# A four-layer hybrid trunk in split float32r: products regrouped by stationary weight, and mixer B's glu and value columns in shared slabs

## The chip, the cores and the metric

The kernel runs on one core of one Trainium2 chip. The metric is the device time of one execution in microseconds, the median over runs; lower is better. TensorE (PE) multiplies, VectorE (DVE) and ScalarE (ACT) work from SBUF and PSUM, GpSimd (POOL) works from SBUF, and the DMA queues bring the weights from HBM. PSUM has eight banks of 512 float32 columns.

## What is computed

The trunk has four residual layers over 256 tokens of 2048 features: mixer A (dilated windowed attention), B (gated convolution), C (retention), then A again, and a closing RMSNorm. The large products are the input and output projections.

```python
for i in range(4):                       # kinds A, B, C, A
    h = rmsnorm(x, norm_w[i])
    x = x + mixer(h)
# mixer B
val, glu_gate, gate = split(h @ w_in, 3)          # 2048 columns each
c = causal_conv31(val * sigmoid(glu_gate)) + conv_b
y = (silu(layernorm(c)) * silu(gate)) @ w_out
```

Mixer A forms q, k (both turned by a rotary table) and v for three dilation groups of eight heads of 128, takes a banded softmax, multiplies by silu(gate) and projects out. Mixer C forms q, k, v and a gate for eight heads, runs a chunked decaying recurrence, normalises each head and projects out.

## The kernel before

**Precision.** Every weight and every activation that enters a projection is split in two float32r parts, high and low (`wh`, `wl`; `xh`, `xl`). A product of two such operands is three matmuls: high by high, high by low, low by high. Each matmul has a weight load of its own (LDWEIGHTS, "PEld" in the profile).

**The stream of slabs.** The weights are read once, as 368 slabs of 1 MB. A `Piece` (L46) is one slab with its matmuls. The main loop (L1064 to the end of the loop) walks the slabs in order: the slab's matmuls, then `cut(i + 2)` (L1049: ACT copies `raw` to `wh` at L1058, DVE or POOL subtracts to `wl` at L1059, and the load of the slab three on is issued by SP at L1047), then the slab's eviction `after`, then side work out of the queues `side`, `slow` and `rare`. `pop` (L114) lets side work in up to a budget in microseconds per slab. Since the program order of every engine is this order, an instruction that waits holds up whatever was written behind it on its engine.

**Three ways to multiply.** `mm_ws` (L137) keeps a 128x128 block of W stationary and streams the 256 tokens, feature-major result, two blocks in a bank; `chunk_ws` and `group_ws` use it (matmuls at L153, L154, L155). `mm_xs` (L175) keeps x stationary and streams 512 weight columns, one bank for each half of the tokens (L187 to L189). `mm_xs2` (L158) keeps x stationary and streams 256 weight columns, both token halves in one bank (L168, L170, L171); only mixer B's first 16 slabs use it.

**PSUM.** `ps_acc` (L65) has four tiles of one bank, `ps_s` and `ps_t` two each.

**Mixer A, q and k.** `after_qk` (L475) evicts two heads with one DVE product by the per-token 1/rms (L479), shuffles the 32 rotary rows (L481), and POOL does the rotation in three steps (L482, L483, L484). After the last k chunk of a head pair, `attention` pushes seven groups of side work; the first of them, after the next slab's matmuls, multiplies q by k (L498 for the first dilation group, L501 for the others).

**Mixer B.** 48 slabs of input projection: for pairs 0 to 3 two 256-wide glu slabs and two 256-wide value slabs each, for pairs 4 to 7 512-wide ones, two pairs at a time; then 16 gate slabs. The eviction of the glu part applies a sigmoid (L684, ACT), that of the value part multiplies (L694, DVE, put in `slow`), `turn` (L672) transposes on PE (L677) and ACT copies to a padded buffer (L678). `conv` (L710) then pushes 31 taps for each pair as side work: tap 0 on ACT (L724), taps 1 to 30 on DVE (L726), each tap one instruction for each of two feature blocks `j`. The accumulators lie in PSUM:

```python
st["ps"] = [(ps_t if c % 2 else ps_s)() for _ in range(2)]
acc = [b[:, 0:S] for b in st["ps"]]      # one bank for each j
...
V.scalar_tensor_tensor(acc[j], src, w, acc[j], op0=OP.mult, op1=OP.add)
```

The budget (L27, 4.7 us; 5.5 in most gate slabs) admits six, later seven taps for each slab. From slab 6 to 45 POOL makes `wl`. When pair 7 is convolved, a LayerNorm over the features follows (L786 to L827: sums on PE at L792, moments, then eight steps that make the operands `big` of the output projection), and the 16 output slabs (`group_ws`) start when the first of these are there. `defer_first` (L226) puts the statistics of the layer's RMSNorm behind the first chunk and that chunk's eviction behind the next slab.

**Residual.** `new_x` (L280) adds a branch of 256 features to x with one DVE instruction (L282) and splits the result for the next layer.

## Time and profile before

| what | value |
|---|---|
| median of 3 runs | 2276.22 us (2275.72 to 2276.3) |
| profiled execution, from first to last instruction | 2275.0 us (its own run time is not recorded) |
| PE busy | 2219.7 us, 98% of the span, 14996 matmuls |
| DVE busy | 1330.0 us, 58% |
| ACT busy | 980.6 us, 43% |
| POOL busy | 553.0 us, 24% |
| DMA | 395.95 MB, mean 174 GB/s |
| granted TensorE clock, mean over the span | 0.994 |

A busy share is a mean over the stages. The layers follow one another: A to about 576 us, B to about 969, C to about 1727, A to the end. PE's matmuls overlap in the records (a 256-column one shows 0.28 us), so their cost is read from the distance between the starts of neighbours, not from their durations. The granted clock has two levels here, 1.00 (2.4 GHz) and 0.50 (1.2 GHz).

### The profile page before, as it was taken

To read this page: it belongs to the slowest core of one execution; us is meant where nothing else is said; L and a number is where in the kernel's file an instruction comes from. 1 tells how busy PE (TensorE), PEld (TensorE's weight loads), DVE (VectorE), ACT (ScalarE), POOL (GpSimd) and SP (SyncE) were. 2 spreads that over 40 slices of the span, in tenths; PEclk is the share of its full clock that TensorE was granted. 3 is DMA by queue.
4 is the path that set the end of the run, shared out by engine and by line. 5 is a ranking of instruction groups with operands and counts; after the bars stand their busy time and mean duration, and the time that the engine had idled before them with its cause. 6 is when DMAs were issued, how large, how long until landed. Compare 5 with 4: busy or idle time off the path is not lost.

```text
span 2275.0 us, 34524 instructions
## 1 busy us (share of the span) xinstructions
PE 2219.7 (98%) x14996; PEld 2059.6 (91%) x14996; DVE 1330.0 (58%) x1536; ACT 980.6 (43%) x913; POOL 553.0 (24%) x273
## 2 busy tenths in 40 slices
PE   6999999999999997999999999999999999999998
PEld 5889999999998887999889889899988889999996
DVE  5545655556597886565455455455555446555554
ACT  4433333345434444444443444344366333333353
POOL 3004344321488973110000000000000005334311
PEclk9999999999999998999999999999999999999999
DMA  6655455445555553555565555555555555455444
GB/s 194 199 198 186 149 167 167 149 148 186 167 185 185 180 172 127 189 182 177 173 201 171 193 181 167 192 183 169 190 169 170 197 187 184 149 167 165 154 145 148
DMA packets 301376, 395.95 MB, mean 174 GB/s; under 512 B 6567, under 2 KB 212775, under 8 KB 301221
## 3 DMA queue, kind: packets, MB, share of 16 engines
q1 hardware_dynamic: 299232, 391.14, 52.7%
q8 instruction: 117, 1.92, 0.4%
q10 hardware_dynamic: 1592, 1.93, 0.2%
q0 software_dynamic: 400, 0.67, 0.2%
q14 instruction: 35, 0.28, 0.0%
HBM read 391.63 MB, written 2.10 MB: 173 GB/s over the span
## 4 chain that ended last, share of the span: by engine, by line
PE 91%; DVE 3%; POOL 2%; DMA 2%; ACT 1%; issue 1%; SPq 0%; DVEq 0%; ACTq 0%; POOLq 0%
PE ps_acc L155 16%; PE ps_acc L154 16%; PE ps_acc L153 16%; PE ps_acc L188 11%; PE ps_acc L187 11%; PE ps_acc L189 11%; PE ps_acc L171 1%; PE ps_acc L168 1%; PE ps_acc L170 1%; PE ps_t L534 1%; POOL tmp L483 1%; DMA xin<-in_x_dram 1%; DVE wl L1059 1%; PE ps_t L969 1%; DMA raw<-in_a_w_in_dram 1%
## 5 line engine op out<-in xcount | busy, mean ns | idle before, releaser
L1059 DVE TENSOR_TENSOR wl<-raw,wh 128x2048 fp32r<-128x2048 f32 (+1 forms) x329 | 781.8, 2378 | 567.1 <-ACT wh L1058 564.8
L1058 ACT ACTIVATE wh<-raw 128x2048 fp32r<-128x2048 f32 (+1 forms) x371 | 703.4, 1898 | 716.6 <-PE ps_acc L154 342.0
L153 PE MATMUL ps_acc<-xhl,wh 128*128 128x256 f32 x2304 | 656.9, 285 | 0.0
L154 PE MATMUL ps_acc<-xhl,wh 128*128 128x256 f32 x2304 | 651.9, 283 | 0.1
L155 PE MATMUL ps_acc<-xhl,wl 128*128 128x256 f32 x2304 | 652.0, 283 | 0.0
L187 PE MATMUL ps_acc<-wh,xhl 128*128 128x512 f32 x1152 | 453.0, 393 | 0.0
L188 PE MATMUL ps_acc<-wl,xhl 128*128 128x512 f32 x1152 | 449.8, 390 | 0.4 <-DVE wl L1059 0.4
L189 PE MATMUL ps_acc<-wh,xhl 128*128 128x512 f32 x1152 | 449.8, 390 | 0.0
L154 PEld LDWEIGHTS ps_acc<-xhl,wh 128*128 128x128 f32 x2304 | 442.0, 192 | 0.7 <-DVE xhl L306 0.3
L153 PEld LDWEIGHTS ps_acc<-xhl,wh 128*128 128x128 f32 x2304 | 442.0, 192 | 0.4
L155 PEld LDWEIGHTS ps_acc<-xhl,wl 128*128 128x128 f32 x2304 | 441.8, 192 | 0.0
L189 PEld LDWEIGHTS ps_acc<-wh,xhl 128*128 128x128 f32 x1152 | 217.1, 188 | 45.9
L188 PEld LDWEIGHTS ps_acc<-wl,xhl 128*128 128x128 f32 x1152 | 217.4, 189 | 44.6 <-DVE wl L1059 0.7
L187 PEld LDWEIGHTS ps_acc<-wh,xhl 128*128 128x128 f32 x1152 | 217.3, 189 | 44.1
L1059 POOL TENSOR_TENSOR wl<-raw,wh 128x2048 fp32r<-128x2048 f32 x42 | 194.7, 4637 | 69.7 <-ACT wh L1058 53.4
L482 POOL TENSOR_TENSOR qk<-qk,ropeA 32x512 f32<-32x512 f32 x48 | 63.6, 1326 | 607.5 <-DVE tmp L481 607.5
L274 POOL COPY ssq<-tmp 128x512 f32<-128x512 f32 x4 | 5.4, 1352 | 836.1 <-ACT tmp L299 812.5
L153 PE MATMUL ps_acc<-z,wh 128*128 128x256 f32 x512 | 145.4, 284 | 0.0
L155 PE MATMUL ps_acc<-z,wl 128*128 128x256 f32 x512 | 145.1, 283 | 0.0
L154 PE MATMUL ps_acc<-z,wh 128*128 128x256 f32 x512 | 144.6, 282 | 0.0
L483 POOL TENSOR_TENSOR tmp<-tmp,ropeA 32x512 f32<-32x512 f32 x48 | 121.0, 2520 | 0.0
L726 DVE SCALAR_TENSOR_TENSOR ps_s<-u,bw,ps_s 128x256 f32<-128x256 f32 x232 | 91.8, 481 | 26.2 <-ACT ps_s L724 26.2
(227 smaller groups left out, 2596.7 us busy)
## 6 DMA issues: line engine op xcount, KB each, us to landing
raw<-in_a_w_in_dram SPq DMA_DIRECT2D x160, 1024.0 KB
raw<-in_c_w_in_dram SPq DMA_DIRECT2D x96, 1024.0 KB
raw<-in_b_w_in_dram SPq DMA_DIRECT2D x48, 1024.0 KB
raw<-in_c_w_out_dram SPq DMA_DIRECT2D x32, 1024.0 KB
raw<-in_a_w_out_dram SPq DMA_DIRECT2D x16, 1024.0 KB
raw<-in_b_w_out_dram SPq DMA_DIRECT2D x16, 1024.0 KB
xin<-in_x_dram SPq DMA_DIRECT2D x16, 128.0 KB
out_dram<-qk SPq DMA_DIRECT2D x8, 256.0 KB
```

The source lines that it names most:

```text
L153: T.matmul(ps, w_h, xh, start=st, stop=False, skip_group_check=True)
L154: T.matmul(ps, w_h, xl, start=False, stop=False, skip_group_check=True)
L155: T.matmul(ps, w_l, xh, start=False, stop=last and i == kk - 1, skip_group_check=True)
L168: T.matmul(ps, xh, wh[:, i, :], start=p == 0 and t == 0 and i == 0, stop=False, skip_group_check=True)
L187: T.matmul(ps, xh, wh[:, i, :], start=p == 0 and i == 0, stop=False)
L188: T.matmul(ps, xh, wl[:, i, :], start=False, stop=False)
L189: T.matmul(ps, xl, wh[:, i, :], start=False, stop=p == np_ - 1 and i == kk - 1)
L482: G.tensor_tensor(q[:32], q[:32], ropeA[:, 0:1].to_broadcast([32, 2, S]), op=OP.mult)
L483: G.tensor_tensor(sw, sw, ropeA[:, 1:2].to_broadcast([32, 2, S]), op=OP.mult)
L726: V.scalar_tensor_tensor(ct[:, j] if k == TAPS - 1 else acc[j], src, w, acc[j], op0=OP.mult, op1=OP.add)
L1058: A.activation(wh[:, sl], r[:, sl], AF.Copy)
L1059: (V if p.lo == "v" else G).tensor_tensor(wl[:, sl], r[:, sl], wh[:, sl].bitcast(F32), op=OP.subtract)
```

## The change

`mm_ws` streams both parts of x in one 512-column matmul against the stationary high weight block, into a whole bank (high by high in the left half, high by low in the right), and then the high part of x in a 256-column matmul against the low weight block, into the right half. The two halves are added on eviction: `joined` copies the right half with ACT and adds the left with DVE; `new_x` adds both halves to x with two DVE instructions. `ps_acc` becomes two tiles of two banks. q is no longer multiplied by the 1/rms in `after_qk` (k still is); the factor goes into the scale of the softmax's exponential. `group_ws`, used by mixer B's output projection alone, keeps three 256-column matmuls as `mm_wg`, with the K tiles outermost in its first slab.

In mixer B, `mm_xs2` goes: every pair has four slabs of 512 columns, 256 of value beside 256 of glu, loaded by two DMAs each. `turn` takes its bank from `ps_s`, `conv` has both accumulators of a pair in one bank of `ps_t`, and the first pair's eviction moves behind slab 4.

```diff
     def ps_acc():
-        return psum.tile([128, 512], F32, name="ps_acc", tag="acc", bufs=4)
+
+        return psum.tile([128, 1024], F32, name="ps_acc", tag="acc", bufs=2)
...
+    def mm_ws(np_, p, kts, hold, xs):
+
+
         def f(wh, wl):
             if p == 0:
-                hold["ps"] = [ps_acc() for _ in range(nb)]
+                hold["ps"] = ps_acc()
             last = p == np_ - 1
             kk = len(kts)
-            order = [(nt, i) for nt in range(2 * nb) for i in range(kk)]
+            order = [(nt, i) for nt in range(2) for i in range(kk)]
             if hold.get("kouter") and p == 0:
-                order = [(nt, i) for i in range(kk) for nt in range(2 * nb)]
+                order = [(nt, i) for i in range(kk) for nt in range(2)]
+            for nt, i in order:
+                x2 = xs(kts[i])
+                ps = hold["ps"][:, nt * 512:(nt + 1) * 512]
+                w_h = wh[:, i, nt * 128:(nt + 1) * 128]
+                w_l = wl[:, i, nt * 128:(nt + 1) * 128]
+                T.matmul(ps, w_h, x2, start=p == 0 and i == 0, stop=False, skip_group_check=True)
+                T.matmul(ps[:, S:2 * S], w_l, x2[:, 0], start=False, stop=last and i == kk - 1,
+                         skip_group_check=True)
+        return f
+
+    def mm_wg(np_, p, kts, hold, xs):
+
+        def f(wh, wl):
+            if p == 0:
+                hold["ps"] = ps_acc()
+            last = p == np_ - 1
+            kk = len(kts)
+            order = [(nt, i) for nt in range(4) for i in range(kk)]
+            if p == 0:
+                order = [(nt, i) for i in range(kk) for nt in range(4)]
...
+                acc = ps_acc()
+                hold["ps"] = [acc[:, 0:512], acc[:, 512:1024]]
...
+    def halves(ps):
+
+        p4 = ps.rearrange("p (n h t) -> p n h t", n=2, h=2)
+        return p4[:, :, 0], p4[:, :, 1]
+
+    def joined(dst, ps):
+        l_, r_ = halves(ps)
+        A.activation(dst, r_, AF.Copy)
+        V.tensor_tensor(dst, l_, dst, op=OP.add)
+
     def x_of(kt):
-        return XHL[kt // 2][:, kt % 2, 0], XHL[kt // 2][:, kt % 2, 1]
+        return XHL[kt // 2][:, kt % 2]
...
+        cols = c0 if isinstance(c0, tuple) else (c0,)
         np_ = nk // 4
         for p in range(np_):
             kts = list(range(p * 4, p * 4 + 4))
-            pieces.append(Piece(wslab(w, p * 4, 4, c0, 512), 4, 512, mm_xs(np_, p, kts, hold, xs),
+            pieces.append(Piece([wslab(w, p * 4, 4, c, 512 // len(cols)) for c in cols], 4, 512,
+                                mm_xs(np_, p, kts, hold, xs),
...
-        V.tensor_tensor(X[c], v3(ps), X[c], op=OP.add)
+
+
+        for part in ps:
+            V.tensor_tensor(X[c], part, X[c], op=OP.add)
...
                 q = lt([128, 2, S], F32, "qk", 8)
                 QK[g, w, hp] = q
-                V.tensor_tensor(q, v3(ps), row2(rstd_p), op=OP.mult)
+                joined(q, ps)
+                if w == 1:
+                    V.tensor_tensor(q, q, row2(rstd_p), op=OP.mult)
                 sw = tmp([128, 2, S])[:32]
...
-                V.tensor_scalar(stt[:, 1:2], stt[:, 0:1], -scale, None, op0=OP.mult)
-                A.activation(p, p, AF.Exp, bias=stt[:, 1:2], scale=scale, accum_out=stt[:, 2:3])
+                V.tensor_scalar(stt[:, 1:2], stt[:, 0:1], qs_[:, 2 + qt:3 + qt], None, op0=OP.mult)
+                A.activation(p, p, AF.Exp, bias=stt[:, 1:2], scale=qs_[:, qt:qt + 1], accum_out=stt[:, 2:3])
...
-                V.tensor_tensor(g, v3(ps), row2(rstd_p), op=OP.mult)
+                joined(g, ps)
+                V.tensor_tensor(g, g, row2(rstd_p), op=OP.mult)
...
-        s1, s2 = norm_stats(first, True, True)
+        s1, s2_ = norm_stats(first, True, True)
+
+        def s2():
+
+            s2_()
+            qs_ = st["qs"] = lt([128, 4], F32, "qs")
+            V.tensor_scalar(qs_[:, 0:2], rcol, 128.0 ** -0.5, None, op0=OP.mult)
+            V.tensor_scalar(qs_[:, 2:4], rcol, -(128.0 ** -0.5), None, op0=OP.mult)
...
-                chunk_ws(wo, c * 256, 8, lambda ps, c=c: new_x(c, ps, next_layer, False), xs=z_of,
+                chunk_ws(wo, c * 256, 8, lambda ps, c=c: new_x(c, halves(ps), next_layer, False), xs=z_of,
...
-        def turn(src, dst, bank=ps_acc):
-            """token-major [128, t, 256 features] to feature-major [128, j, tokens]."""
-            ps = bank()
+        def turn(src, dst):
+
+            ps = ps_s()
             for j in range(2):
                 for t in range(2):
                     T.transpose(ps[:, j * S + t * 128:j * S + (t + 1) * 128], src[:, t, j * 128:(j + 1) * 128], ident)
             A.activation(dst, v3(ps), AF.Copy)

-        def after_glu(c, n):
+        def after_pair(c):
+
             def f(ps):
-                sg = lt([128, 2, 512], F32, "sg", 2)[:, :, :256 * n]
+                sg = lt([128, 2, 512], F32, "sg", 2)[:, :, 0:256]
                 for t in range(2):
-                    A.activation(sg[:, t], tok(ps, t), AF.Sigmoid, scale=rcol[:, t:t + 1])
-                ln["sg", c] = sg
-            return f
-
-        def after_val(c, n):
-            def f(ps):
-                sg = ln.pop(("sg", c))
+                    A.activation(sg[:, t], ps[t][:, 256:512], AF.Sigmoid, scale=rcol[:, t:t + 1])

                 def m_():
                     for t in range(2):
-                        V.scalar_tensor_tensor(sg[:, t], tok(ps, t), rcol[:, t:t + 1], sg[:, t],
+                        V.scalar_tensor_tensor(sg[:, t], ps[t][:, 0:256], rcol[:, t:t + 1], sg[:, t],
                                                op0=OP.mult, op1=OP.mult)

-                def t_(e):
+                def t_():
                     u = lt([128, 2, PAD + S], F32, "u", 5)
                     G.memset(u[:, :, 0:PAD], 0.0)
-                    turn(sg[:, :, e * 256:(e + 1) * 256], u[:, :, PAD:])
-                    conv(c + e, u)
+                    turn(sg, u[:, :, PAD:])
+                    conv(c, u)
                 if c == 0:
                     m_()
                 else:
                     slow.append(m_)
-                for e in range(n):
-                    slow.append(lambda e=e: t_(e))
+                slow.append(t_)
             return f

         def conv(c, u):
...
-                        st["ps"] = [(ps_t if c % 2 else ps_s)() for _ in range(2)]
-                    acc = [b[:, 0:S] for b in st["ps"]]
+                        st["ps"] = v3(ps_t())
+                    acc = [st["ps"][:, j] for j in range(2)]
...
-        for c in range(NARROW_PAIRS):
-            chunk_ws(wi, 2048 + c * 256, KT, after_glu(c, 1), before=open_scope(f"b{L}") if c == 0 else None,
-                     lo=lo, budget=B_BUDGET, mm=mm_xs2)
-            chunk_ws(wi, c * 256, KT, after_val(c, 1), lo=lo, budget=B_BUDGET, mm=mm_xs2)
-        defer_first(n0, s1, s2)
-        for c in range(NARROW_PAIRS, 8, 2):
-            chunk_xs(wi, 2048 + c * 256, KT, after_glu(c, 2), lo=lo, budget=B_BUDGET)
-            chunk_xs(wi, c * 256, KT, after_val(c, 2), lo=lo, budget=B_BUDGET)
+        for c in range(8):
+            chunk_xs(wi, (c * 256, 2048 + c * 256), KT, after_pair(c), lo=lo, budget=B_BUDGET,
+                     before=open_scope(f"b{L}") if c == 0 else None)
+        defer_first(n0, s1, s2, 3)
...
-                V.tensor_tensor(m1, v3(ps), st["rope"][:, 0:1].to_broadcast([128, 2, S]), op=OP.mult)
-                V.tensor_tensor(m2, v3(ps), st["rope"][:, 1:2].to_broadcast([128, 2, S]), op=OP.mult)
+                joined(m1, ps)
+                V.tensor_tensor(m2, m1, st["rope"][:, 1:2].to_broadcast([128, 2, S]), op=OP.mult)
+                V.tensor_tensor(m1, m1, st["rope"][:, 0:1].to_broadcast([128, 2, S]), op=OP.mult)
...
-            nc.sync.dma_start(raw[i], p.src)
+            n = p.n // len(p.src)
+            for j, src in enumerate(p.src):
+                nc.sync.dma_start(raw[i][:, :, j * n:(j + 1) * n], src)
```

## Rows read from the trace of the kernel before

**Rows 1.** The page: the chain that ended last, shares of the span by engine
```profile
PE 91%; DVE 3%; POOL 2%; DMA 2%; ACT 1%; issue 1%; SPq 0%; DVEq 0%; ACTq 0%; POOLq 0%
```
**Rows 2.** Timeline of PE, weights stationary: start us, us, engine, line, operation, out<-in
```profile
299.82 0.28 PE L155 MATMUL ps_acc<-xhl,wl 128*128 128x256 f32 x1
...
302.94 0.28 PE L154 MATMUL ps_acc<-xhl,wh 128*128 128x256 f32 x1
```
**Rows 3.** Timeline of PE, x stationary
```profile
119.73 0.39 PE L187 MATMUL ps_acc<-wh,xhl 128*128 128x512 f32 x1
...
123.81 0.39 PE L187 MATMUL ps_acc<-wh,xhl 128*128 128x512 f32 x1
```
**Rows 4.** Groups by line and shape: xcount | busy us, mean ns | idle before
```profile
L153 PE MATMUL ps_acc<-xhl,wh 128*128 128x256 f32 x2304 | 656.9, 285 | 0.0
...
L153 PE MATMUL ps_acc<-z,wh 128*128 128x256 f32 x512 | 145.4, 284 | 0.0
...
L153 PE MATMUL ps_acc<-v,wh 128*128 128x256 f32 x128 | 36.2, 283 | 0.0
```
**Rows 5.** Timeline around the end of a last k chunk in mixer A
```profile
315.26 0.69 DVE L479 TENSOR_TENSOR qk<-ps_acc,rstd_p 128x512 f32<-128x512 f32 x1 [1.48 <-PE ps_acc L155]
...
316.80 1.29 POOL L482 TENSOR_TENSOR qk<-qk,ropeA 32x512 f32<-32x512 f32 x1 [5.17 <-DVE tmp L481]
...
321.46 1.25 POOL L484 TENSOR_TENSOR qk<-qk,tmp 32x512 f32<-32x512 f32 x1
322.77 0.49 PE L501 MATMUL ps_s<-qk 128*128 128x128 f32 x2 [1.12 <-POOL qk L484]
```
**Rows 6.** Groups by line and shape: an ACT copy of a whole bank
```profile
L519 ACT ACTIVATE tmp<-ps_t 128x512 f32<-128x512 f32 x32 | 19.0, 594 | 15.7 <-PE ps_t L517 15.7
```
**Rows 7.** Timeline at the start of mixer A's output projection
```profile
533.25 0.69 DVE L562 TENSOR_TENSOR v<-tmp,v 128x512 fp32r<-128x512 f32 x1 [0.70 <-ACT v L561]
...
534.22 0.28 PE L153 MATMUL ps_acc<-v,wh 128*128 128x256 f32 x1
```
**Rows 8.** Timeline of DVE in mixer C's output slabs, and PE's next slab but one
```profile
1206.22 0.68 DVE L282 TENSOR_TENSOR x<-ps_acc,x 128x512 f32<-128x512 f32 x1
...
1211.98 0.37 PE L153 MATMUL ps_acc<-z,wh 128*128 128x256 f32 x1
```
**Rows 9.** Stretch of all taps, line L726 alone: us, DVE busy (x), PEclk, DMA share, GB/s
```profile
613.50:841.30 227.80, 189.83 (x480) 1.00 0.57 183
```
**Rows 10.** Timeline of DVE at the end of the taps
```profile
831.36 6.77 DVE L1059 TENSOR_TENSOR wl<-raw,wh 128x2048 fp32r<-128x2048 f32 x1 [1.76 <-issue]
838.06 2.43 DVE L726 SCALAR_TENSOR_TENSOR ps_t<-u,bw,ps_t 128x256 f32<-128x256 f32 x6
```
**Rows 11.** Timeline of DVE in the LayerNorm: an instruction that reads its predecessor's result
```profile
847.24 0.42 DVE L798 TENSOR_TENSOR tmp<-mu,shift 128x256 f32<-128x256 f32 x1
847.70 0.43 DVE L799 TENSOR_TENSOR tmp<-tmp 128x256 f32<-128x256 f32 x1
```
**Rows 12.** Timeline of ACT: evictions of two token halves from one bank, then from two banks
```profile
612.23 0.84 ACT L684 ACTIVATE sg<-ps_acc,rcol 128x256 f32<-128x256 f32 x2 [3.36 <-PE ps_acc L171]
...
802.82 0.69 ACT L848 ACTIVATE sg<-ps_acc,rcol 128x512 f32<-128x512 f32 x1 [0.75 <-PE ps_acc L189]
805.54 0.69 ACT L848 ACTIVATE sg<-ps_acc,rcol 128x512 f32<-128x512 f32 x1 [2.03 <-PE ps_acc L189]
```
**Rows 13.** Timeline at mixer B's opening
```profile
594.72 0.84 ACT L684 ACTIVATE sg<-ps_acc,rcol 128x256 f32<-128x256 f32 x2 [2.58 <-DVE rcol L269]
```
**Rows 14.** Stretches: us, busy (x) of PE, PEld, DVE, ACT, POOL, then PEclk
```profile
241.00:245.00 4.00, 2.87 (x23) 2.63 (x22) 0.85 (x3) 0.09 (x1) 2.33 (x2) 1.00 0.75 246
867.00:873.50 6.50, 4.74 (x38) 4.24 (x36) 2.69 (x5) 5.51 (x8) 1.81 (x1) 1.00 0.00 0
874.00:880.00 6.00, 3.75 (x17) 3.75 (x18) 2.54 (x2) 0.75 (x2) 6.00 (x4) 0.50 0.43 135
887.30:890.60 3.30, 3.18 (x15) 3.18 (x16) 3.30 (x4) 0.02 (x1) 0.00 (x0) 0.50 0.60 177
```

More of the change, by code (lines that the diff above doesn't have):

```diff
@@ L32 @@
 LN_ON_DVE = 2
-NARROW_PAIRS = 4
 PAD = TAPS - 1
@@ L185, in f @@
                 ps = hold["ps"][t]
-                xh, xl = (v[:, t * 128:(t + 1) * 128] for v in xs(kts[i]))
+                x2 = xs(kts[i])
+                xh, xl = (x2[:, h, t * 128:(t + 1) * 128] for h in range(2))
                 T.matmul(ps, xh, wh[:, i, :], start=p == 0 and i == 0, stop=False)
@@ L198, in wslab, with chunk_ws @@
         return w[kt0 * 128:(kt0 + kk) * 128, c0:c0 + n].rearrange("(k p) n -> p k n", p=128)
-    def chunk_ws(w, c0, nk, after, xs=x_of, kt0=0, before=None, lo=lambda p: "v", budget=3.0, hold=None,
-                 mm=None):
+    def chunk_ws(w, c0, nk, after, xs=x_of, kt0=0, before=None, lo=lambda p: "v", budget=3.0, hold=None):
         hold = {} if hold is None else hold
-        mm = mm or mm_ws
         np_ = nk // 8
@@ L206, in chunk_ws @@
             kts = list(range(p * 8, p * 8 + 8))
-            pieces.append(Piece(wslab(w, kt0 + p * 8, 8, c0, 256), 8, 256, mm(np_, p, kts, hold, xs),
-                                after=(lambda: after(hold["ps"][0])) if p == np_ - 1 else None,
+            pieces.append(Piece([wslab(w, kt0 + p * 8, 8, c0, 256)], 8, 256, mm_ws(np_, p, kts, hold, xs),
+                                after=(lambda: after(hold["ps"])) if p == np_ - 1 else None,
                                 before=before if p == 0 else None, lo=lo(p), budget=budget))
@@ L219, in done @@
                     for b in range(2):
-                        after(c0 // 256 + 2 * e + b, holds[e]["ps"][b])
-                pieces.append(Piece(wslab(w, p * 4, 4, c0 + e * 512, 512), 4, 512,
-                                    mm_ws(np_, p, kts, holds[e], xs, nb=2),
+                        after(c0 // 256 + 2 * e + b, holds[e]["ps"][:, b * 512:(b + 1) * 512])
+                pieces.append(Piece([wslab(w, p * 4, 4, c0 + e * 512, 512)], 4, 512,
+                                    mm_wg(np_, p, kts, holds[e], xs),
                                     after=done if p == np_ - 1 else None,
@@ L851, in t_ @@
                     GT[c + e] = lt([128, 2, S], F32, "big", 18)
-                    turn(sg[:, :, e * 256:(e + 1) * 256], GT[c + e], ps_s if c == 6 else ps_acc)
+                    turn(sg[:, :, e * 256:(e + 1) * 256], GT[c + e])
                 for e in range(2):
@@ L883, in layer_b @@
         for g in range(2):
[L884 removed]
+            group_ws(wo, g * 1024, KT, lambda c, ps: new_x(c, [v3(ps)], next_layer, False), z_of,
                      before=ready if g == 0 else None, budget=5.0,
@@ L1018, in outp @@
                 nl = next_layer if p == 3 else None
-                chunk_ws(wo, c * 256, 8, lambda ps, c=c, nl=nl: new_x(c, ps, nl, True), xs=z_of, kt0=8 * p,
+                chunk_ws(wo, c * 256, 8, lambda ps, c=c, nl=nl: new_x(c, halves(ps), nl, True), xs=z_of, kt0=8 * p,
                          before=(lambda: ensure(need)) if c == 0 else None, hold={"kouter": c == 0 and p == 3})
```

32 lines of the change are left out of this document (6 added, 26 removed).

## The prediction

> **What bounds the kernel now.** I read the page's chain first: 91% of the span is PE's own work [rows 1]. So I next read what one product costs PE, then the few places where PE waits, then, for mixer B, how near DVE is to taking over. One measure serves throughout: the distance between the starts of neighbouring matmuls. With weights stationary, 26 distances of 256 columns take 3.12 us, 0.1200 each [rows 2]; with x stationary, 18 distances of 512 columns take 4.08 us, 0.2267 each [rows 3]. Twice the columns cost 0.1067 more, so about 13.3 ns of each matmul does not depend on its columns. That is what regrouping can save. The profiled span is 2275.0 us, 1.2 below the median 2276.2; I make the sum on the span and carry it over to the median.
>
> **The change, part by part.**
>
> *Products.* A set of three matmuls costs 3 x 0.1200 = 0.3600 us; as one of 512 and one of 256 columns 0.2267 + 0.1200 = 0.3467, a saving of 13.3 ns. The sets of `mm_ws` outside mixer B are 2304 + 512 + 128 = 2944 [rows 4]: **-39.2 us**. Here the Trainium skill differs ("TensorE: Matmul & The Clock Gate", "Back-to-back issue gap"): it gives a warm distance of columns / 2.4 plus 2.5 ns, and by it the saving is 2.5 ns a set, 7.4 us in all. Its 109 ns for 256 columns does not agree with the 120 measured, so the rows decide.
>
> *k and q in mixer A.* After a last k chunk the chain is DVE eviction, shuffle, three POOL steps, and PE waits 1.12 us for the end of it [rows 5]. It occurs once for each head pair, 8 times in the two A layers. The new eviction is an ACT copy (0.59 [rows 6]), a handoff (0.07), a DVE add (0.69, as the present product), 0.035 until a dependent instruction can start [rows 11], and the product (0.69): 1.39 longer. Behind it in DVE's queue is the next slab's low part, and POOL, which shares the stretch with it, is pushed back whole. PE meanwhile is there earlier, since its 16 sets are 0.21 shorter. Each wait grows by 1.6 to about 2.8 us: **+12.8**. For q the longer eviction has most of a chunk to hide in.
>
> *The clock in these waits.* In the stretch of a present wait, 2.87 of 4.00 us busy, the clock stays at 1.00; it fell to 0.50 after a stretch in which PE lacked 1.8 of 6.5 us, and stayed low at least 3.3 us at a time [rows 14]. The new waits lie on the wrong side of these two. At the low level 256 columns take 3.18 / 15 = 0.212 us, so each fall costs about 3.4 x (1 - 0.120 / 0.212) = 1.5 us. Bounds: 0, and 8 x 3.0 = 24 if each lasts twice as long. I take five falls of eight: **+7.5**.
>
> *Output projection of the first layer.* The last low part of the operand ends at 533.94, 0.28 before PE reads it [rows 7]. Its eviction, a gate, gets the same 1.39 and the twelve sets ahead shrink by 0.16: **+1.3**.
>
> *Costs hidden.* Adding halves costs C's evictions and `new_x` one more DVE instruction of 0.69. With two accumulator tiles instead of four, the eviction must be done before the next slab but one. In the tightest place it starts at 1206.22; with two adds it ends at 1207.6, and PE needs the tile at 1211.98 [rows 8]. If that cover of 4 us went, PE would wait for the eviction itself, up to 1.4 us a chunk. Softmax scales, the second load of each slab on SP and the K order of B's first output slab I cost at nothing: the first two are a few instructions on queues with idle time, the third only reorders products that wait for the LayerNorm.
>
> *Mixer B.* Sharing slabs turns 768 matmuls of 256 columns into 384 of 512, 5.1 us of PE. But the taps must be looked at. DVE works on them for 227.8 us, 189.8 of it busy, 480 instructions [rows 9]; six of them take 2.43 with 0.48 for the last, a distance of 0.39 [rows 10]. They overlap because neighbours use different banks: a tap waits only for the one two before it. The change puts both in one bank. What does a bank do to waits here? Where two token halves share a bank, both evictions start together after the slab's end, at 612.23, with ACT idle for 3.36 before; where they have two banks, the first starts 2.7 us ahead of the second [rows 12]. So waits on PSUM go by the bank, not by the columns. Within DVE, an instruction that waits for its predecessor starts 35 ns after its end [rows 11]. If the rule by bank holds within DVE too, each tap costs 0.480 + 0.035 = 0.515: 247 us for 480. With 5.5 for the glu products between them and 4 for the low part made near the end (6.77 in rows 10, beside POOL work that will be over by then) and a microsecond gained at the last pair of each, the stretch is 256 us, 28 longer. It starts about 3.5 earlier: five slabs shorter by 0.32, and a first tap that no longer stands behind slab 5's sigmoid, though PE, and slab 5 queued behind, waits some 2 us for the first transpose, which now directly follows sigmoid (0.84 [rows 13]) and product. The LayerNorm waits for the last tap, the output projection for the LayerNorm, so **+24.4** from a stage in which PE's 5.1 us no longer count. Bounds for one tap: 0.39 (no new wait) and 0.52.
>
> Sum: -39.2 + 12.8 + 7.5 + 1.3 + 24.4 = +6.8 us, **2283 us**.
>
> **The rivals.**
>
> *The taps keep their distance.* Nothing in the profile shows two DVE instructions on one bank; the evidence by bank is PE against ACT. Then B stays paced by PE: -5.1 for the slabs, +2.1 for the first transpose, about -1 because supply to the taps is smoother, and the sum is -39.2 - 5.1 + 12.8 + 7.5 + 1.3 + 2.1 - 1 = -21.6: **2254 us**, faster. The point from which it decides: at six taps a slab a pair takes 31 / 6 slabs of 5.44 us and a turn of 0.4, 28.5 in all; 60 taps and a product of 0.8 fill that at 0.46 a tap. Below, the taps are free; above, each 0.01 is 4.8 us. The Trainium skill speaks for this rival ("PSUM — Partial Sum Buffer", "PSUM bank collisions raise a hardware error"): the compiler ties two instructions on one bank when they are on different engines, which would leave DVE's own alone. The rows with PE and ACT agree; no row here has two DVE instructions on one bank.
>
> *The clock holds.* With the taps tied but no fall in the eight waits: +6.8 - 7.5 = -0.7, **2275 us**, no change. For it: every present wait of this kind is passed at 1.00. Against it: the new ones are more than twice as long.
>
> *The product saves nothing*: a 512-column product of two blocks of 256 might pay 13.3 ns for each block. Then the first term is zero: about **2322 us**. The 512-column rows speak against it, but they stream weights, not x.
>
> **How the numbers follow.** Taps tied and some falls of the clock 0.50 (own range 2276 to 2292); taps tied, clock holds 0.18; taps free 0.25 (2245 to 2263); product saves nothing 0.03; something else 0.04. The likeliest is 2283. A range that leaves out no more than two in ten must reach into the free taps: 2249 to 2292. About 0.2%, 4.6 us, is what a measurement of this kernel can tell from no change. Faster by more than that: nearly all of the free taps and a little of the second case, 0.30. Within it: a third of the first case and most of the second, 0.29. Slower: the rest of the first and the small cases, 0.41.
>
> **What would show it.** Set pitch: starts at 0.227 and 0.120 in turn. Mixer A: eight waits of L501's successor on POOL near 2.8 us, and stretches at 0.50 behind some. Mixer B: the 480 taps at 0.515 instead of 0.39, a tap stretch near 256 us, and PE waiting for the glu product before transposes. If the taps show 0.39, the step on the bank is wrong and the time is near 2254; if the tap stretch is as forecast but the time is below 2270, I have missed cover at the LayerNorm.

## The result, and the profile after

The changed kernel takes **2306.89 us** (median of 4 runs, 2304.62 to 2309.24) beside 2276.26 for the kernel before on the same chip: a ratio of 1.0134, 95% interval 1.0122 to 1.0146. It is 30.6 us slower. The forecast was 2283 (2249 to 2292): the sign was right, the size was not, and the time lies outside the range. The profiled execution of the changed kernel spans 2305.6 us, that of before 2275.0; the ledger below is made between these two.

First the page of the changed kernel: the chain that ended last, shares of the span by engine and then by line.

```profile
PE 79%; DVE 12%; ACT 3%; POOL 2%; issue 2%; DMA 2%; SPq 0%; DVEq 0%; ACTq 0%; POOLq 0%
PE ps_acc L153 27%; PE ps_acc L154 14%; PE ps_acc L194 10%; PE ps_acc L195 10%; PE ps_acc L193 10%; DVE ps_t L746 8%; PE ps_acc L176 1%; PE ps_acc L175 1%; PE ps_acc L174 1%; PE ps_t L555 1%; POOL qk L503 1%; ACT wh L1077 1%; DMA xin<-in_x_dram 1%; DVE wl L1078 1%; PE ps_t L986 1%
```

Before, PE held 91% of it [rows 1]. Now the taps of mixer B's convolution (L746) are on it with 8%. Next the stretches of the changed kernel, cut where the work on PE changes: the start, mixer A's products with stationary weights, its output projection, mixer B up to its output projection, that and mixer C, the second A up to its end on PE, and the tail. Columns: stretch and us, busy time (and instructions) of PE, PEld, DVE, ACT, POOL, then the granted clock, the DMA share and GB/s.

```profile
0.00:166.20 166.20, 144.92 (x646) 118.61 (x647) 88.09 (x96) 68.60 (x66) 20.26 (x22) 0.99 0.61 196
166.20:533.40 367.20, 355.38 (x2081) 312.15 (x2080) 219.63 (x236) 158.13 (x160) 133.29 (x72) 0.99 0.48 159
533.40:580.00 46.60, 45.55 (x258) 39.30 (x257) 34.46 (x37) 26.43 (x32) 14.25 (x7) 1.00 0.61 197
580.00:888.30 308.30, 283.39 (x1236) 230.83 (x1234) 268.73 (x522) 129.93 (x122) 217.55 (x73) 0.97 0.49 161
888.30:1747.00 858.70, 846.81 (x4566) 734.55 (x4567) 503.94 (x430) 399.25 (x375) 33.91 (x22) 0.99 0.54 180
1747.00:2292.40 545.40, 533.32 (x2887) 459.18 (x2886) 306.12 (x298) 233.99 (x226) 142.66 (x80) 0.99 0.49 164
2292.40:2305.60 13.20, 0.42 (x2) 0.00 (x0) 5.15 (x14) 3.48 (x8) 0.00 (x0) 0.71 0.47 160
```

The same stretches of the kernel before took 166.6, 363.2, 46.1, 282.3, 864.6, 542.3 and 9.9 us. So the differences are -0.4, +4.0, +0.5, **+26.0**, -5.9, +3.1 and +3.3: together +30.6. Mixer B came out near its term of +24.4. The surprise is in the other rows: stretches that were to gain from the new products gained little or lost.

Why, PE's groups by line and shape begin to say: count, busy us and mean ns, then the idle time before them and what ended it.

```profile
L153 PE MATMUL ps_acc<-xhl,wh 128*128 128x512 f32 x2304 | 822.8, 401 | 0.0
L154 PE MATMUL ps_acc<-xhl,wl 128*128 128x256 f32 x2304 | 647.3, 281 | 0.0
...
L555 PE MATMUL ps_t<-tmp,v 128*128 128x128 f32 x256 | 34.5, 278 | 3.7 <-ACT tmp L540 3.6
...
L522 PE MATMUL ps_s<-qk 128*128 128x128 f32 x128 | 22.0, 285 | 20.1 <-POOL qk L505 20.1
...
L703 PE MATMUL ps_s<-ident,sg 128*128 128x128 f32 x64 | 12.1, 293 | 14.0 <-DVE sg L715 12.2 <-ACT sg L868 1.4
...
L812 PE MATMUL ps_s<-big,ones 128*128 128x256 f32 x4 | 2.1, 674 | 11.0 <-DVE big L746 11.0
```

The eight waits for rope (L522: q times k waits for the last step of the rotary turn on POOL, L505) idle 20.1 us; the same group of before had 9.0, eight times the 1.12 of [rows 5]. L703 waits 12.2 us for glu products and L812 11.0 for the last tap: that is mixer B. And L555, the product of probabilities and v, waits 3.6 us for the turned probabilities; before it waited for nothing, and the prediction has no term for it.

A 512-column product of [rows 3] lasts 0.39 us; here the mean is 0.401. The distance between starts is the better measure. Two undisturbed stretches of PE in the changed kernel, first and last row of each:

```profile
298.87 0.40 PE L153 MATMUL ps_acc<-xhl,wh 128*128 128x512 f32 x1
...
304.53 0.40 PE L153 MATMUL ps_acc<-xhl,wh 128*128 128x512 f32 x1
...
369.95 0.39 PE L153 MATMUL ps_acc<-xhl,wh 128*128 128x512 f32 x1
...
375.14 0.40 PE L153 MATMUL ps_acc<-xhl,wh 128*128 128x512 f32 x1
```

Sixteen sets take 5.66 us in the first, 0.354 each, and fifteen take 5.19 in the second, 0.346. The forecast of 0.3467 holds in one kind of stretch, and in the other half of the saving is gone. Over the 2304 sets with x at full clock a set takes 353 ns, where the three products of before took 362 with the same gaps at slab ends counted: about 9 saved, not 13.3 (with z about 8, with v 6).

The clock, in six stretches behind waits of the changed kernel (columns as above):

```profile
243.20:246.60 3.40, 3.40 (x12) 2.92 (x12) 1.57 (x5) 1.95 (x3) 0.00 (x0) 0.50 0.10 33
325.10:328.50 3.40, 3.40 (x13) 2.92 (x12) 1.28 (x4) 2.71 (x3) 0.00 (x0) 0.50 0.00 0
403.70:407.00 3.30, 3.17 (x11) 2.78 (x12) 1.29 (x5) 1.35 (x3) 0.08 (x1) 0.50 0.23 78
1700.80:1704.00 3.20, 3.20 (x11) 2.71 (x11) 2.03 (x3) 2.43 (x3) 0.00 (x0) 0.50 0.34 115
1960.20:1963.40 3.20, 3.20 (x12) 2.71 (x12) 1.36 (x5) 2.42 (x3) 0.00 (x0) 0.50 0.01 3
2226.30:2229.60 3.30, 3.30 (x16) 3.11 (x15) 0.92 (x5) 2.82 (x4) 0.00 (x0) 0.50 0.00 0
```

Four of them follow rope waits, the fifth follows L555's second wait (2226.3), and one stands at the end of mixer C (1700.8), behind a wait for its last gate. Six sets in 3.40 us would have taken 2.11 at full clock, so a fall costs about 1.3 us.

### The profile page after: what moved, and what is told of

It reads as the page before. It is cut to its first block, busy times and chain, and to the rows that moved or that the text cites. A ratio compares the mean times of both kernels' runs of the same rounds, so it can differ in the third digit from the quotient of the medians.

```text
span 2305.6 us, 28188 instructions
## 1 busy us (share of the span) xinstructions
PE 2209.8 (96%) x11668; PEld 1894.6 (82%) x11668; DVE 1426.1 (62%) x1632; ACT 1019.8 (44%) x989; POOL 561.9 (24%) x273
## 4 chain that ended last, share of the span: by engine, by line
PE 79%; DVE 12%; ACT 3%; POOL 2%; issue 2%; DMA 2%; SPq 0%; DVEq 0%; ACTq 0%; POOLq 0%
PE ps_acc L153 27%; PE ps_acc L154 14%; PE ps_acc L194 10%; PE ps_acc L195 10%; PE ps_acc L193 10%; DVE ps_t L746 8%; PE ps_acc L176 1%; PE ps_acc L175 1%; PE ps_acc L174 1%; PE ps_t L555 1%; POOL qk L503 1%; ACT wh L1077 1%; DMA xin<-in_x_dram 1%; DVE wl L1078 1%; PE ps_t L986 1%
## 5 line engine op out<-in xcount | busy, mean ns | idle before, releaser
L153 PE MATMUL ps_acc<-xhl,wh 128*128 128x512 f32 x2304 | 822.8, 401 | 0.0
L153 PEld LDWEIGHTS ps_acc<-xhl,wh 128*128 128x128 f32 x2304 | 436.1, 189 | 102.3
L193 PE MATMUL ps_acc<-wh,xhl 128*128 128x512 f32 x1280 | 504.2, 394 | 0.0
L194 PE MATMUL ps_acc<-wl,xhl 128*128 128x512 f32 x1280 | 500.8, 391 | 1.1 <-DVE wl L1078 1.1
L195 PE MATMUL ps_acc<-wh,xhl 128*128 128x512 f32 x1280 | 500.7, 391 | 0.0
L195 PEld LDWEIGHTS ps_acc<-wh,xhl 128*128 128x128 f32 x1280 | 241.8, 189 | 50.9
L193 PEld LDWEIGHTS ps_acc<-wh,xhl 128*128 128x128 f32 x1280 | 242.2, 189 | 49.8
L746 DVE SCALAR_TENSOR_TENSOR ps_t<-u,bw,ps_t 128x256 f32<-128x256 f32 x464 | 227.2, 490 | 19.9 <-ACT ps_t L744 4.2
L153 PE MATMUL ps_acc<-z,wh 128*128 128x512 f32 x512 | 182.3, 397 | 0.0
L153 PEld LDWEIGHTS ps_acc<-z,wh 128*128 128x128 f32 x512 | 96.9, 189 | 22.2
L205 ACT ACTIVATE qk<-ps_acc 128x512 f32<-128x512 f32 x48 | 28.7, 598 | 156.7 <-PE ps_acc L154 156.7
L154 PEld LDWEIGHTS ps_acc<-z,wl 128*128 128x128 f32 x512 | 97.0, 190 | 0.2
L301 DVE TENSOR_TENSOR x<-ps_acc,x 128x512 f32<-128x512 f32 x88 | 60.4, 691 | 43.7 <-PE ps_acc L154 35.7
```

The source lines that it names most:

```text
L153: T.matmul(ps, w_h, x2, start=p == 0 and i == 0, stop=False, skip_group_check=True)
L154: T.matmul(ps[:, S:2 * S], w_l, x2[:, 0], start=False, stop=last and i == kk - 1, skip_group_check=True)
L193: T.matmul(ps, xh, wh[:, i, :], start=p == 0 and i == 0, stop=False)
L194: T.matmul(ps, xh, wl[:, i, :], start=False, stop=False)
L195: T.matmul(ps, xl, wh[:, i, :], start=False, stop=p == np_ - 1 and i == kk - 1)
L205: A.activation(dst, r_, AF.Copy)
```

## The experiments

**Two tiles for the taps.** The accumulators go back to a tile each; nothing else is touched.

```diff
-                        st["ps"] = v3(ps_t())
-                    acc = [st["ps"][:, j] for j in range(2)]
+                        st["ps"] = [ps_t() for _ in range(2)]
+                    acc = [b[:, 0:S] for b in st["ps"]]
```

> The changed kernel with one edit: the two accumulators of the convolution's taps stand in two PSUM tiles (two banks) again, not in the halves of one. Theory (the shared tile makes each tap wait for the one before): the distance of taps falls from 0.525 to about 0.39 us, and the stretch from mixer B's first product to its output projection's first falls from 308.3 us (580.04 to 888.34) to 278-286, so the time is 2277-2285 us. A little of it may be lost where the first tap of a pair, an ACT copy, must wait for the last tap of the pair before: up to 1.2 us each, seven times. Rival (the loss comes from the shared slabs: at each pair PE stands about 2 us before the transposes, behind the glu product): the taps are at 0.39 but the stretch stays over 295 us, and the time over 2294 us.

Measured: 2279.56 us, ratio to the kernel before 1.0009 (1.0000 to 1.0019). The stretch of all taps, L746 alone (us, DVE busy and count, clock, DMA), in the changed kernel:

```profile
614.70:871.40 256.70, 233.63 (x480) 0.97 0.49 160
```

and in this one:

```profile
613.35:841.95 228.60, 189.50 (x480) 1.00 0.55 180
```

A run of taps in the timeline of DVE (start, us, count at the end), in the changed kernel:

```profile
837.92 29.36 DVE L746 SCALAR_TENSOR_TENSOR ps_t<-u,bw,ps_t 128x256 f32<-128x256 f32 x56
```

and in this one:

```profile
701.49 18.89 DVE L746 SCALAR_TENSOR_TENSOR ps_t<-u,bw,ps_t 128x256 f32<-128x256 f32 x48
```

Without the last tap's own 0.49 the first is 55 distances of 0.525 us, the second 47 of 0.391. Two groups of this kernel on PE show what became of the waits:

```profile
L703 PE MATMUL ps_s<-ident,sg 128*128 128x128 f32 x64 | 10.2, 276 | 3.1 <-DVE sg L715 1.6 <-ACT sg L868 1.4
...
L812 PE MATMUL ps_s<-big,ones 128*128 128x256 f32 x4 | 1.0, 379 | 0.0
```

The waits for glu products fall from 12.2 to 1.6 and the one for the last tap from 11.0 to nothing; the stretch from B's first product to the output projection's first is 280.1 us. So the waits at the pairs were not the shared slabs' own: the product stood in DVE's queue behind slow taps. The rival falls. Against the 282.3 of before, what is left of B's change is worth 2.2 us.

**Tile or bank?** Edit to the kernel *before*: odd pairs get one tile that spans two banks, even pairs one tile in one bank.

```diff
-                        st["ps"] = [(ps_t if c % 2 else ps_s)() for _ in range(2)]
-                    acc = [b[:, 0:S] for b in st["ps"]]
+                        if c % 2:
+                            b = ps_w()
+                            st["ps"] = [b[:, 0:S], b[:, 512:512 + S]]
+                        else:
+                            b = ps_s()
+                            st["ps"] = [b[:, 0:S], b[:, S:2 * S]]
+                    acc = st["ps"]
```

(`ps_w` is a tile of 1024 columns that takes the place of the two `ps_t` tiles while mixer B runs.)

> The kernel before with one edit in mixer B: for pairs with an even number both accumulators of the taps stand in one tile of one bank, for pairs with an odd number in one tile that spans two banks, one accumulator in each. Theory A (a tap waits by PSUM bank): even pairs at 0.515-0.525 us a tap, odd pairs at 0.39. Theory B (a tap waits by tile, whatever its banks; the late evictions in the tail of the changed kernel, where two banks were one tile, speak for it): both at 0.525. Theory C (neither; something else of the changed kernel tied them): both at 0.39.

Its timeline of DVE, an even pair (`ps_s`) and then an odd one (`ps_t`):

```profile
614.32 24.12 DVE L738 SCALAR_TENSOR_TENSOR ps_s<-u,bw,ps_s 128x256 f32<-128x256 f32 x46 [13.08 <-ACT ps_s L736]
...
646.21 16.76 DVE L738 SCALAR_TENSOR_TENSOR ps_t<-u,bw,ps_t 128x256 f32<-128x256 f32 x32
```

(24.12 - 0.49) / 45 = 0.525, and (16.76 - 0.49) / 31 = 0.525. Theory B: the accumulators have a bank each in the odd pairs and are tied all the same. What ties neighbouring taps is that they share a tile. This one edit takes the kernel before to 2308.1 us in a single run, 32.0 above the 2276.16 beside it: the whole loss of the change can be had without any of its products.

**The last k chunk by three products.** A function `mm_w3`, the old order of three 256-column products into the first bank, is used for the chunk that stands before the scores.

```diff
-                joined(q, ps)
-                if w == 1:
-                    V.tensor_tensor(q, q, row2(rstd_p), op=OP.mult)
+                if g == 2 and w == 1:
+                    V.tensor_tensor(q, v3(ps[:, 0:512]), row2(rstd_p), op=OP.mult)
+                else:
+                    joined(q, ps)
+                    if w == 1:
+                        V.tensor_tensor(q, q, row2(rstd_p), op=OP.mult)
...
-                    chunk_ws(wi, g * A_GCOLS + w * 1024 + hp * 256, KT, af)
+                    chunk_ws(wi, g * A_GCOLS + w * 1024 + hp * 256, KT, af,
+                             mm=mm_w3 if g == 2 and w == 1 else None)
```

> The changed kernel with one edit: the last k chunk of each head pair in mixer A (8 chunks of 32 sets) is made by three 256-column products in one bank and evicted by one DVE product with 1/rms, as before the change. Theory (the copy and the add in the eviction lengthen the wait for rope, and the longer wait brings the clock down): the eight waits in the score products fall from 2.61-2.72 to about 1.3 us (-11), the four stretches at clock 0.50 behind them go (-6), and 256 sets cost 9 ns more each (+2.3): 2292 us. Rival 1 (what lengthens the wait is the next slab's low part in front of the chain, or POOL): the waits stay over 2 us and the time over 2300. Rival 2 (the clock falls for another reason than the longer wait): the waits fall but the stretches at 0.50 stay, about 2298.

Measured: 2297.22 us, ratio 1.0090 (1.0075 to 1.0105), 9.7 below the changed kernel. The group of the score products:

```profile
L544 PE MATMUL ps_s<-qk 128*128 128x128 f32 x128 | 21.6, 281 | 9.9 <-POOL qk L527 9.9
```

and the stretches behind two of the eight waits (the clock column is 1.00 behind all eight):

```profile
244.80:248.20 3.40, 3.30 (x19) 2.94 (x20) 1.56 (x5) 1.79 (x3) 0.05 (x1) 1.00 0.59 205
...
2186.00:2189.40 3.40, 3.32 (x19) 2.95 (x20) 1.56 (x5) 1.81 (x3) 0.03 (x1) 1.00 0.58 203
```

The waits go from 20.1 to 9.9 us, and with them go the four falls of the clock. Both rivals fall. In the profiled run the first 169.2 us, where the change does nothing, took 3 us more than in the changed kernel's, and the clock was low there for 10.2 us instead of 3.4; that is part of the 5 us by which the expected 2292 was missed.

**The last gate, and the tail.** The fourth gate chunk of each A layer with `mm_w3`, and in the last closing chunk a tile of its own for the second token half:

```diff
-                hold["ps"] = [acc[:, 0:512], acc[:, 512:1024]]
+                hold["ps"] = [acc[:, 0:512], ps_t() if own else acc[:, 512:1024]]
```

> The changed kernel with two edits at places far from each other: in mixer A the last gate chunk of each layer is made by three 256-column products and evicted by one DVE product; and in the last chunk of the closing projection the second token half accumulates in a PSUM tile of its own. Theory: the last softmax stands in DVE's and ACT's queues behind the gate, whose eviction is longer by a copy that waits behind a high part and an add that waits behind a low part; so PE's waits of 1.9 and 2.0 us for the probabilities at 510.6 and 2223.7 go, the wait of 1.2 at the start of the first layer's output projection too, and the fall of the clock at 2226.3. In the tail the first token half's eviction begins about 2.7 us before the last matmul ends and not after it, and the end comes about 2.7 us earlier. Together 2307 - 5.1 - 1.5 - 2.7 + 0.6 for the 64 sets = 2298 us. Rival: PE waits there because its products are shorter, not because the gate is later: the waits of 1.9 and 2.0 stay, only the tail moves, 2304 us.

Measured: 2304.58 us, ratio 1.0121 (1.0105 to 1.0138). The tail of the changed kernel, last matmul and first eviction, and then of this one:

```profile
2292.43 0.39 PE L195 MATMUL ps_acc<-wh,v 128*128 128x512 f32 x1
2292.92 0.75 DVE L650 TENSOR_TENSOR qk<-ps_acc,x 128x256 f32<-128x256 f32 x2 [9.84 <-PE ps_acc L195]
```

```profile
2290.88 0.76 DVE L673 TENSOR_TENSOR qk<-ps_acc,x 128x256 f32<-128x256 f32 x2 [7.05 <-PE ps_acc L213]
...
2293.18 0.40 PE L213 MATMUL ps_t<-wh,v 128*128 128x512 f32 x1
```

The first eviction moves from behind the last matmul to 2.3 us ahead of its start; from the end of PE to the last of DVE it is 5.0 us, not 7.8 (5.1 before the change). The wait at the start of the first output projection (1.05 us at 538.95) is gone too. But the group of L555 still idles 3.8 us: the fourth gate is not what it waits behind, so that part of the theory failed.

**The second gate, then all gates.** By the timeline of the changed kernel, what ends L555's first wait is ACT's copy of the turned probabilities (L540), and the eviction in front of that copy is the one of the *second* gate chunk:

```profile
505.74 0.57 ACT L205 ACTIVATE g<-ps_acc 128x512 f32<-128x512 f32 x1
505.87 2.29 DVE L1078 TENSOR_TENSOR wl<-raw,wh 128x2048 fp32r<-128x2048 f32 x1 [1.12 <-ACT wh L1077]
...
508.08 0.68 DVE L206 TENSOR_TENSOR g<-ps_acc,g 128x512 f32<-128x512 f32 x1
508.80 0.69 DVE L572 TENSOR_TENSOR g<-g,rstd_p 128x512 f32<-128x512 f32 x1
...
512.01 0.59 ACT L540 ACTIVATE tmp<-ps_t 128x512 f32<-128x512 f32 x1
...
512.66 1.16 PE L555 MATMUL ps_t<-tmp,v 128*128 128x128 f32 x8 [1.74 <-ACT tmp L540]
```

ACT's copy of the gate (L205) is done at 506.31, but DVE's low part of 2.29 us stands before the add (508.08), the add puts the product 0.72 us later (508.80), and the copy stands in ACT's queue behind the whole gate, so that it begins at 512.01. So a combined version took the two tiles, the k chunks, the tail, and `mm_w3` for the second and fourth gate:

```diff
-                joined(g, ps)
-                V.tensor_tensor(g, g, row2(rstd_p), op=OP.mult)
+                if hp in (1, 3):
+                    V.tensor_tensor(g, v3(ps[:, 0:512]), row2(rstd_p), op=OP.mult)
+                else:
+                    joined(g, ps)
+                    V.tensor_tensor(g, g, row2(rstd_p), op=OP.mult)
```

> The changed kernel with the accumulators of the taps in two tiles, the last k chunk of each head pair and the second and fourth gate chunk of each mixer A layer as three 256-column products with one eviction, and the second token half of the last closing chunk in a tile of its own. If the losses add: 2279.6 (two tiles alone) - 9.7 (k) - 2.3 (fourth gate and tail) = 2267.6; if also the waits of 1.9 and 2.0 us for the last softmax belong to the second gate's longer eviction (theory after the fourth gate left them in place), they go and with them a fall of the clock, - 5.5 + 0.6: 2262.7 us, against 2276.4 before. Rival (PE meets that softmax early because its products are shorter, whatever the gate does): the waits stay near 2 us and the time at 2267 or more.

Measured: 2261.74 us, ratio 0.9937 (0.9923 to 0.9951): faster than both kernels. The time is within 1 us of the expected 2262.7, in part by luck: that sum took L555's waits to go, and they shrink from 3.6 us to 1.6. L555 waits less, but not nothing; with the condition dropped, so that all four gates are evicted in one step, it does:

> The combined version of before with one more edit: all four gate chunks of each mixer A layer as three 256-column products with one eviction, not the second and fourth alone. Two waits for the last softmax are left in the combined version, 1.03 us at 504.6 and 0.89 at 2181.5. Theory (the first gate's longer eviction pushes the softmax before it, and so the rest, back on DVE and ACT): both fall under 0.3 us. Rival (PE is there earlier because its products up to that point are shorter): both stay near 0.9 us. Four chunks of 32 sets cost 1.2 us, so the time itself is 2260.5 to 2263 either way.

The group in the combined version, then in the one with all gates (2260.1 us, a single run):

```profile
L577 PE MATMUL ps_t<-tmp,v 128*128 128x128 f32 x256 | 34.1, 276 | 1.6 <-ACT tmp L562 1.6
```

```profile
L577 PE MATMUL ps_t<-tmp,v 128*128 128x128 f32 x256 | 33.7, 274 | 0.0
```

With all gates evicted in one step PE waits for nothing. In mixer A's order the third gate comes behind these waits, so the first gate's longer eviction was the other half. The rival falls: counted from the last rope wait, the copy that PE waits for is 1.0 us earlier than in the combined version (26.7 us against 27.7), and PE itself, whose first gate has longer products again, only 0.2 later (27.7 against 27.5).

**What a set costs: groups of eight, one width, groups of sixteen.** Three kernels ask why a set takes 346 ns here and 354 there. The first puts the eight high products of a feature tile before its eight low ones:

```diff
-                T.matmul(ps[:, S:2 * S], w_l, x2[:, 0], start=False, stop=last and i == kk - 1,
-                         skip_group_check=True)
...
+                elif i == kk - 1:
+                    for m in range(kk):
+                        T.matmul(ps[:, S:2 * S], wl[:, m, nt * 128:(nt + 1) * 128], xs(kts[m])[:, 0],
+                                 start=False, stop=last and m == kk - 1, skip_group_check=True)
```

> The changed kernel with one edit: in a slab with stationary weights the eight 512-column products of a feature tile come first and then its eight 256-column products, instead of the two in turn (slabs with K outermost stay as they are). It tells apart why a set takes 346.7 ns in some stretches of the changed kernel and 353 in others, where 226.7 + 120.0 = 346.7 was forecast. Theory A (the turn from one width to the other costs the difference): 512-column products follow each other at 227 and 256-column ones at 120, a set is 346.7 everywhere, and the time is about 2816 x 4 ns = 11 us shorter, 2296 us. Theory B (a 512-column product with x moving is itself longer than one with weights moving): 512-column products stand at 230-236 still, the set stays at 350-353, 2305-2309 us.

The second makes the low product 512 wide:

```diff
-                T.matmul(ps[:, S:2 * S], w_l, x2[:, 0], start=False, stop=last and i == kk - 1,
+                T.matmul(ps, w_l, x2, start=False, stop=last and i == kk - 1,
```

> The changed kernel with one edit: the product of the low weight part is also 512 columns wide, over both parts of x (it adds the product of the two low parts, which the kernels leave out), so that stationary-weight slabs hold 512-column products only. Theory A (a mixture of widths costs the extra time of a set): every such product takes 227 ns, as where weights move. Theory B (a 512-column product with x moving has two lengths by itself): they take 231-236, two of them 460-470 ns. The time is longer by about 2944 x 0.11 = 320 us either way.

The third is the combined version with all sixteen high products of a slab first (`high` and `low` issue the two products of the set):

```diff
-            for nt, i in order:
...
+                for part in (high, low):
+                    for nt, i in order:
+                        part(nt, i)
```

> The combined version of before (two tiles, three products in some k and gate chunks, own tile in the tail) with one more edit: in stationary-weight slabs all sixteen 512-column products come first and then all sixteen 256-column ones. With groups of eight the distances were 229 to 236 ns for the first five 512-column products behind a switch of width and 227 to 230 after, 115 for the first 256-column one and 120 after: 24 ns more for eight sets than 8 x 346.7. Theory (the price hangs on the switch of width): 24 / 16 = 1.5, a set of 348.2 ns instead of about 351 in turn, 1920 sets of the in-projections: -5 us, 2256.5. Rival (it hangs on something else, the group only coincides): sets stay at 350 to 351, and the time at 2261.7 within 2.

Measured: 2307.12 us for the first, ratio 1.0136 (1.0121 to 1.0151), no change from the changed kernel; 2595.89 for the second; **2253.8** for the third, ratio 0.9902 (0.9885 to 0.9918). PE's timeline of the first, eight and eight:

```profile
200.06 2.00 PE L153 MATMUL ps_acc<-xhl,wh 128*128 128x512 f32 x8
201.91 1.12 PE L159 MATMUL ps_acc<-xhl,wl 128*128 128x256 f32 x8
202.86 2.00 PE L153 MATMUL ps_acc<-xhl,wh 128*128 128x512 f32 x8
```

of the second, one width alone:

```profile
302.87 0.39 PE L153 MATMUL ps_acc<-xhl,wh 128*128 128x512 f32 x1
...
307.18 0.39 PE L154 MATMUL ps_acc<-xhl,wl 128*128 128x512 f32 x1
```

and of the third, sixteen and sixteen:

```profile
200.55 3.82 PE L149 MATMUL ps_acc<-xhl,wh 128*128 128x512 f32 x16
204.20 2.08 PE L153 MATMUL ps_acc<-xhl,wl 128*128 128x256 f32 x16
206.12 0.63 PE L149 MATMUL ps_acc<-xhl,wh 128*128 128x512 f32 x2
```

Eight sets take 2.80 us, 0.350 each. With one width, 19 distances take 4.31, 0.227 each. Sixteen sets take 5.57, 0.348 each. Averaged by place over the 28 groups of the third that stand between groups of their own kind, the 512-column products behind a switch are 233, 236, 228, 232 and 231 ns apart and 227 from the sixth on; the 256-column ones 113, 119 and then 120. The groups of eight show the same at the same places. So a switch of width disturbs the products behind it, and the two switches of a group together cost about 20 ns, shared by eight sets or by sixteen. In the changed kernel each set has two switches, yet pays 0 to 7 ns and not 20; nothing there has time to settle, but why it pays so much less is not shown. Theory A of the first experiment was too simple, for groups of eight spend five of their eight 512-column products settling; theory B fell with the second kernel, though only for x: in mixer C's output slabs (z) that kernel keeps 228 to 241, and there grouping gave nothing either, 128 sets taking 49.0 us in turn and 49.1 in sixteens.

The first kernel's time did not show the shorter sets: with their gaps they take 352 ns against 353, about 3 us in all, and its first 169 us took 3 us more, with the clock low for 10.2 us instead of 3.4. Its clock fell behind six rope waits instead of four, but not at the two other places of the changed kernel. That the third gained 7.9 us and not 5 is partly its own clock: no fall at the end of mixer C, and in the start 3.4 us of low clock where the combined version has 10.2.

## Why the forecast was wrong

| term | forecast | found |
|---|---|---|
| products, 2944 sets | -39.2 | -26 |
| rope waits | +12.8 | +11.1 |
| clock outside mixer B | +7.5 | +7.7 |
| start of the first output projection | +1.3 | +1.2 |
| mixer B | +24.4 | +26.0 |
| softmax waits at L555 | 0 | +4.0 |
| tail | 0 | +2.7 |
| closing projection, wait at the end of C | 0 | +2.0 |

These sum to +28.7; 1.9 us of the 30.6 stay unassigned. The forecast's sum was +6.8, so it was 23.8 us too low: 13 of them lie in the products, and 8.7 in the last three rows, which it had at nothing.

**The products: the step that failed.** The prediction took a set as a 512-column distance with one kind of operand and a 256-column distance with another, each from a stretch of one width, and added them. Both figures are right where widths don't alternate: 0.227 and 120.0 ns are what the long groups settle to. No row of before had two widths in turn, and the prediction gave the sum no bounds but 0 in a rival. In turn a set takes 353 ns and not 346.7, so the term is -26 us and not -39.2: the runs with groups and with one width show that it is the turn from one width to the other that costs, for x. The Trainium skill ("TensorE: Matmul & The Clock Gate", "Back-to-back issue gap") says columns / 2.4 plus 2.5 ns warm, and says it of one matmul in isolation, which the prediction left out. By that the set saves 2.5; the changed kernel saves 9 a set, and the settled distances of these runs agree with the 13.3, not with the 2.5.

**k, q and the clock: right, in part by luck.** A rope wait is 20.1 / 8 = 2.51 us against 1.12, longer by 1.39 where 1.6 was forecast (and 1.12 + 1.6 is 2.7, not the 2.8 that the prediction names). Counted from the start of the k chunk's last product, POOL's first step begins 1.34 us later (3.21 against 1.87), near the 1.39 worked out from [rows 5, 6, 11]. POOL's three steps then take 5.77 us instead of 5.90, which was not foreseen, and PE is there 0.10 to 0.21 us earlier, as foreseen. The clock fell at four of the eight waits, where five were expected, and at 1.3 us each, where 1.5 was; two falls elsewhere made up the sum, so that the term came out is luck. How many of the eight bring the clock down is not settled by the wait alone: with waits of the same length it fell behind two in the kernel with two tiles, three in the one with the last gate and the tail, and six in the groups of eight.

**The taps: right in size, wrong in the reason.** Distance 0.525 (0.515 forecast; the tap itself takes 490 ns here instead of 480), stretch 256.7 us (256), start 2.9 us earlier against B's own start (3.5). That the stretch agrees to a microsecond is luck: 480 taps at 0.525 are 252 us, 5 more than forecast, and what stands between them came to 5 us where 8.5 was taken. But the rule "by bank", read from [rows 12], is wrong: the two-bank tile shows that it is the tile. The rows with PE and ACT had both at once, one tile in one bank and two tiles in two. The Trainium skill ("PSUM — Partial Sum Buffer", "PSUM bank collisions raise a hardware error") asks to guard by bank between engines; here instructions of one engine wait for each other, over two banks of one tile too, and of waits on DVE alone that section does not speak. The rival that kept the taps' distance read it as leaving DVE alone; that fell.

**The tail and the end of C: the same mistake at two other places.** With "by bank", the closing chunk's two halves, in two banks of what had become one tile, would still be evicted one after the other. By tile they wait for the last matmul: +2.7 us. The end of mixer C shows it once more. The two halves of its last gate, before and then in the changed kernel:

```profile
1673.12 0.69 ACT L940 ACTIVATE g<-ps_acc,rcol 128x512 f32<-128x512 f32 x1
1674.43 0.69 ACT L940 ACTIVATE g<-ps_acc,rcol 128x512 f32<-128x512 f32 x1 [0.63 <-PE ps_acc L189]
```

```profile
1697.58 1.27 ACT L957 ACTIVATE g<-ps_acc,rcol 128x512 f32<-128x512 f32 x2 [1.33 <-PE ps_acc L195]
```

Before, the first half was evicted 0.9 us ahead of the start of the last product (1674.01); now both come behind it, PE waits there 1.9 us instead of 1.2, and the clock falls (1700.8). No run takes these halves apart.

**Costs hidden at nothing.** The extra adds in C and `new_x` and the second load of a slab are hidden, as said: none ends a wait of PE in the changed kernel's groups. The two accumulator tiles are hidden as far as their number goes, but not their two banks, as the tail and the end of C show. The gate's eviction was costed for the output projection's start alone; what stands behind it in ACT's queue, the copy of the turned probabilities, was not followed. That is the +4.0 at L555 (3.6 of idle time, the rest a slower start behind it); the fall of the clock behind its second wait is counted with the clock.

**What stays open.** Why some undisturbed stretches in turn keep 346 ns and others 354, so that the forecast's 346.7 holds in one of them, and why the z products of mixer C don't settle. And why the closing projection, whose 192 products are all 512 wide with the same operands as before, takes 44.6 us in the changed kernel and in the one-width kernel alike, where it took 43.3 before.

## What to carry to other kernels

Count waits by the tile that the program allots, not by the bank under it: accumulators that take turns, and halves that are evicted apart, want tiles of their own. When an eviction gets longer, follow what stands behind it in the queues of both its engines, not only who reads its result. And products of two widths can be worth grouping: with x they gave 9 ns a set in turn and about 12 in groups of sixteen (360 - 348), with z grouping gave nothing; and what the regrouping saves is only kept where no short wait is fed by the longer eviction.

## What the runs showed that was not expected

- A matmul's distance depends on those some five products back: behind a change from 256 to 512 columns the first five stand 228 to 236 ns apart before they settle to 227, behind the opposite change the first is 113 before 120.
- The tie of the taps alone, put into the kernel before, costs 32 us in a single run, as much as the whole change.
- The clock fell behind four of eight waits of 2.5 us (behind two to six of eight in the other runs with such waits) and behind none of eight of 1.2 us (9.9 / 8), with the same work around them.
